# Odd token tiles of the third output-projection part placed between the even tiles of the last part, with both last weight tiles in T3's place

## The chip, the core and the metric

The kernel runs on one core of one Trainium2 chip. The metric is the device time of one execution in microseconds. The kernel before takes 1251.24 us (median of three runs, 1250.85 to 1251.51). In the texts PE is the matrix engine, PEld its weight loads, ACT the scalar engine, DVE the vector engine, POOL the third elementwise engine, and SP the engine on whose queue every DMA is issued.

## What is computed

One decoder layer over 1024 tokens of width 1024, in float32. Cut to what matters here:

```python
mix = jnp.concatenate([oa.reshape(B, S, DIL_WIDTH),
                       ob.reshape(B, S, DIFF_WIDTH)], axis=-1)   # two attentions, 512 columns each
x = x + mix @ w_out[l]                    # output projection, residual
h = rmsnorm(x, g_ffn[l])
gate, up = jnp.split(h @ w_gate_up[l], 2, axis=-1)
x = x + (jax.nn.silu(gate) * up) @ w_down[l]
return rmsnorm(x, g_final)
```

## The kernel before

Every float32 product is done as three products of rounded parts: an operand is split into `h` (rounded) and `l` (the rest), and `h*h + h*l + l*h` is summed in PSUM. A split is a cast on ACT followed by a subtraction on POOL or DVE.

**Output projection.** The 1024 rows of `w_out` are taken in four parts of two 128-row blocks, named by their first block: 4, 6, 0 and 2, in that order. For each part, `mix_tiles` holds the attention's output (`mixh`, `mixl`, two of the four buffers of tag `mix`), and `out_weights` loads the weights for one half `n` of the output columns: a DMA into `raw_o` (one buffer), the cast (L136) and the subtraction (L137). `out_proj_group(mix, w, t, n, name)` does one group: six matmuls of 128x512 for token tile `t` and column half `n`, and an addition to the residual `x1[t]` on DVE (L630). There are 16 groups in each part.

The parts 4, 6 and 0 are generators (`out_proj`) whose groups `mixed` strews between the steps of the last two attention pairs as filler for PE. The scheduler then sets each engine's order from its own estimate of time. Part 2 needs the last attention pair, so it stands behind it, in a region whose PE and POOL order is written out by hand (`manual_schedule`): for the token tiles in the order `TOKENS` = 0, 2, 4, 6, 1, 3, 5, 7, two groups (`n` = 0 and 1, named `op_l`), then the RMSNorm of that tile (`norm`), the store of `x1[t]`, and with a lag of two tiles `flip_low`, which transposes a normalised even tile into `hB[1]` and `hB[2]`, operands of the feed-forward part. That part uses Strassen's seven products, T3 being one of them, and `h7` is the place kept for its operand.

**Norm.** `norm` squares and sums the tile on ACT (L159), takes the power -0.5 on POOL (L145), then scales the low half on DVE (L167). The high half of an even tile goes over ACT (L164) and POOL (L165), of an odd one over DVE (L167).

**Memory near the seam.** The pool `h2T` opens when the attention's pools are closed, and lies on their place. In it, `h1`, `h5`, `h2`, `h3` are operands at once, `h4` and `h6` first hold the split weights of the first gate and up products (`ops0`), and `h7` first holds weights of part 2: before the change those of column half 1 (`wo_l1`); those of half 0 are in two of the four buffers of tag `w`, which frees them when part 0 has used them for half 0. `raw0` (`load_raw`, 1 MB each for gate and up, L729) takes two of the four `mix` buffers, those of part 0.

After the loop, `flip_high` transposes odd tiles and the difference tile `t` (L875 on DVE) into `hB[3]` and `hB[5]`, and `gate_up_first` does the first gate and up products (`pa_g`, `pa_u`), four of 12 matmuls each.

Of the kernel before, what the change touches and what calls it, by code (L numbers as in the profile page):

```python
# [13 lines left out]
F32R = mybir.dt.float32r  # L14
# [5 lines left out]
P = 128  # L20
S = 1024
D = 1024
KT = D // P
# [20 lines left out]
TOKENS = (0, 2, 4, 6, 1, 3, 5, 7)  # L44
# [27 lines left out]
def tile_hybrid_block(  # L72
# [17 lines left out]
    nc = tc.nc  # L90
# [12 lines left out]
    def psum(tag, name):  # L103
        return pp.tile([P, 512], F32, tag=tag, bufs=BANKS[tag], name=name)
# [18 lines left out]
    def split_weights(src, a, name, tag="w", eng=None, parts=None):  # L123

        small = tag == "w"
        pool = wp if small else mapp
        raw = pool.tile([P, 1024], F32, tag="raw" if small else "KL", bufs=1 if small else 2, name=f"raw_{name}")
        nc.sync.dma_start(raw.rearrange("p (a b) -> p a b", a=a), src)
        if parts:
            w = parts  # L130
        elif small:
            w = [pool.tile([P, 1024], F32R, tag=tag, bufs=4, name=f"w_{name}_{i}") for i in "hl"]
        else:
            both = pool.tile([P, 2, 1024], F32R, tag=tag, name=f"w_{name}")
            w = [both[:, i, :] for i in range(2)]
        nc.scalar.copy(w[0], raw)  # L136
        (eng or nc.gpsimd).tensor_tensor(w[1], raw, w[0].bitcast(F32), op=ALU.subtract)  # L137
        return [w_.rearrange("p (a b) -> p a b", a=a) for w_ in w]
# [172 lines left out]
    def chain(*gens):  # L311
        for g in gens:
            yield from g
# [32 lines left out]
    for c in range(3):  # L346
        ps = psum("S", f"gps_{c}")
# [212 lines left out]
    def qk_dil(pair, res):  # L560
        return project_qk(QA + pair * P, KA + pair * P, f"a{pair}", res)

    def qk_diff(h, res):
        return project_qk(QB + h * P, KB + h * P, f"d{h}", res)
# [5 lines left out]
    fill = chain(  # L570
        qk_diff(1, qd[1]),
        project_v(VB + 256, False, "d1", vd2),
        qk_diff(2, qd[2]),
        qk_diff(3, qd[3]),
        project_v(VA, True, "a0", va),
        qk_dil(0, qa[0]),
        qk_dil(1, qa[1]),
        project_v(VA + 256, True, "a1", va2),
# [28 lines left out]
    def mix_tiles(k0):  # L607
        return [mxp.tile([P, 2, S], F32R, tag="mix", name=f"mix{w}_{k0}") for w in "hl"]

    def load_mix(tiles, k0, c):  # L610
        for tl, w in zip(tiles, "hl"):
            nc.sync.dma_start(
                tl[:, :, c * 512 : (c + 1) * 512].bitcast(F32),
                mix_d[w, k0, c].rearrange("k p s -> p k s"),
            )

    n_op = [0]

    def out_proj_group(mix, w, t, n, name):

        sl = slice(t * P, (t + 1) * P)
        cols = slice(n * 512, (n + 1) * 512)
        n_op[0] += name == "l"
        ps = psum("PSPSOS"[n_op[0] % 6] if name == "l" else "P", f"op_{name}_{t}_{n}")
        i = 0
        for k in range(2):
            for l_, r_ in ((mix[0], w[0]), (mix[0], w[1]), (mix[1], w[0])):
                mm(ps, l_[:, k, sl], r_[:, k, :], start=i == 0, stop=i == 5)
                i += 1
        nc.vector.tensor_tensor(x1[t][:, cols], ps, x1[t][:, cols], op=ALU.add)  # L630

    def out_weights(k0, n, parts=None):
        return split_weights(w_out_v[:, k0 : k0 + 2, n * 512 : (n + 1) * 512], 2, f"o{k0}_{n}", parts=parts)

    def out_proj(k0, first=False):
        mix = mix_tiles(k0)
        for c in range(2):
            load_mix(mix, k0, c)
        if first:
            for t in TOKENS:  # L640
                x1[t] = xp.tile([P, D], F32, tag="x1t", name=f"x1_{t}")
                nc.sync.dma_start(x1[t], x[0, t * P : (t + 1) * P, :])
        for n in range(2):
            w = out_weights(k0, n)
            for t in range(KT):
                out_proj_group(mix, w, t, n, f"{k0}")
                yield 1.3

    fill = chain(out_proj(4, True), out_proj(6), out_proj(0))
    mixed(a2, fill, 1.0)  # L650
    mixed(attend_dil(3, qa[3], va2[1]), fill, 1.2)
    run_all(fill)
# [12 lines left out]
    h2p = h2_cm.__enter__()  # L665
# [3 lines left out]
    def h2_tile(i):  # L669
        hB[i] = h2p.tile([P, 2, 4, 512], F32R, tag=f"h{i}", name=f"h2_{i}")  # L670

    wo_l1 = None
    for i in (1, 6, 7, 5, 2, 4, 3):
        if i == 7:
            wo_l1 = h2p.tile([P, 4, 1024], F32R, tag=f"h{i}", name="wo_l1")
        elif i in (4, 6):
            ops0[i == 4] = h2p.tile([P, 4, 2, 512], F32R, tag=f"h{i}", name=f"ops0_{i}")
        else:
            h2_tile(i)
# [9 lines left out]
    def split(src, dst, eng):  # L689

        nc.scalar.copy(dst[:, 0], src)  # L691
        eng.tensor_tensor(dst[:, 1], src, dst[:, 0].bitcast(F32), op=ALU.subtract)  # L692
# [33 lines left out]
    def load_raw(p, up):  # L726
        raw = mxp.tile([P, KT, 256], F32, tag="mix", name=f"raw_{'gu'[up]}{p}")
        c0 = up * D_FF + 2 * p * P
        nc.sync.dma_start(raw, w_gu[:, :, c0 : c0 + 256])  # L729
        return [raw[:, 4 * k : 4 * k + 4, m * P : (m + 1) * P] for m in range(2) for k in range(2)]  # L730

    def as_left(op):
        return op.rearrange("p w (k m) -> p w k m", k=4)
# [132 lines left out]
    def flip_low(j):  # L866
        flip(hns[2 * j][:, LO], 1, j, f"b11_{j}")
        flip(hns[2 * j][:, HI], 2, j, f"b21_{j}")
# [15 lines left out]
        g.tensor_tensor(v[:, LO], u[:, LO], v[:, LO], op=ALU.add)  # L884
        g.tensor_tensor(v[:, HI], v[:, HI], v[:, LO], op=ALU.subtract)

    wo = [out_weights(2, 0), out_weights(2, 1, [wo_l1[:, i] for i in range(2)])]
    mix = mix_tiles(2)
    load_mix(mix, 2, 0)
    gf = mid.tile([P, D], F32, tag="gf", bufs=1, name="gf")  # L890
    nc.sync.dma_start(gf, broadcast(g_ffn[0], D))
    load_mix(mix, 2, 1)
    raw0 = [load_raw(0, up) for up in range(2)]
    a0 = [[as_left(ops0[up][:, i]) for i in range(4)] for up in range(2)]
    with tc.manual_schedule(engines={mybir.EngineType.PE, mybir.EngineType.Pool}):
        for i, t in enumerate(TOKENS):
            for n in range(2):
                out_proj_group(mix, wo[n], t, n, "l")
            high = xp.tile([P, D], F32, tag="x1t", name=f"hn_f{t}") if t % 2 else None
            hns[t] = norm(mid, x1[t], gf, t, "f", high)  # L900
            nc.sync.dma_start(x1_d[t], x1[t])
            if 2 <= i < 6:
                flip_low(i - 2)
            if i >= 3 and i < 7:
                split(raw0[0][i - 3], a0[0][i - 3], nc.gpsimd)
        for i in range(4):
            split(raw0[1][i], a0[1][i], nc.gpsimd)
    with tc.manual_schedule(engines={mybir.EngineType.PE}):
        c0 = [block_tile(0, up) for up in range(2)]
        first = [gate_up_first(up, a0[up], c0[up], c0[0] if up else None) for up in range(2)]  # L910
# [88 lines left out]
    for c0 in range(0, NPAIR - 1, 2):  # L999
# [3 lines left out]
        for i in ORDER:  # L1003
# [14 lines left out]
            for tq in range(4):  # L1018
                ps = next_bank(f"d{c0}_{i}_{tq}")
                sl = slice(tq * P, (tq + 1) * P)  # L1020
                n = 0
# [27 lines left out]
    for m, rows in ((0, (2, 3)), (1, (4, 5))):  # L1049
        for tq in range(4):  # L1050
            sl = slice(tq * P, (tq + 1) * P)
            t = 2 * tq + m
# [4 lines left out]
            for n, r in enumerate(rows):  # L1057
                ps = next_bank(f"dl_{t}_{n}")
                i = 0
                for k in range(2):  # L1060
                    a, w = oal[2 * m + k], wl[2 * k + n]
# [44 lines left out]
```

## Time and profile before

| what | us |
|---|---|
| median of the runs | 1251.24 |
| the profiled execution: its time | 1254.24 |
| the profiled execution: its span | 1252.5 |
| PE busy in the span | 1219.6 |
| the last attention matmul on PE, start | 542.08 |
| the first gate product on PE, start | 586.20 |
| the first up product on PE, start | 602.86 |

The profiled execution is 3.0 us longer than the median, and 1.74 us of it lie outside the span. The page's first part gives busy time by engine, the second part the span in 40 slices with the clock that PE was granted (PEclk, as tenths of full speed). The view of waits says which engine sat idle and what ended it; the timeline gives instructions in order of time, those of one kind that follow each other in one row, with the idle time ahead of it in square brackets; the windows give busy time per engine and the granted clock in a chosen stretch.

### The profile page before, as it was taken

To read this page: it belongs to the slowest core of one execution; us is meant where nothing else is said; L and a number is where in the kernel's file an instruction comes from. 1 tells how busy PE (TensorE), PEld (TensorE's weight loads), DVE (VectorE), ACT (ScalarE), POOL (GpSimd) and SP (SyncE) were. 2 spreads that over 40 slices of the span, in tenths; PEclk is the share of its full clock that TensorE was granted. 3 is DMA by queue.
4 is the path that set the end of the run, shared out by engine and by line. 5 is a ranking of instruction groups with operands and counts; after the bars stand their busy time and mean duration, and the time that the engine had idled before them with its cause. 6 is when DMAs were issued, how large, how long until landed. Compare 5 with 4: busy or idle time off the path is not lost. (4 is left out here: it accounts for less than half of the span.)

```text
span 1252.5 us, 18470 instructions
## 1 busy us (share of the span) xinstructions
PE 1219.6 (97%) x6318; PEld 1040.9 (83%) x6318; DVE 785.4 (63%) x1667; ACT 576.4 (46%) x1300; POOL 737.3 (59%) x664
## 2 busy tenths in 40 slices
PE   6999999999999999998999999999999999999996
PEld 5989989988998888876788888888888887888885
DVE  6548688876766587858554455554545535655597
ACT  5346567665765565535433443434343433222214
POOL 2024344354443443426936797889878786956676
PEclk8999999999999999998999999999999999999999
DMA  6232233132213383252232345333544369966633
GB/s 217 67 89 71 62 98 89 42 93 87 83 51 108 118 307 132 85 173 104 84 121 88 145 169 184 135 120 133 185 168 175 129 244 372 403 230 253 220 126 134
DMA packets 99613, 184.63 MB, mean 147 GB/s; under 512 B 6920, under 2 KB 58376, under 8 KB 99520
## 3 DMA queue, kind: packets, MB, share of 16 engines
q1 hardware_dynamic: 99520, 183.46, 41.9%
q8 instruction: 50, 0.82, 0.3%
q14 instruction: 43, 0.35, 0.1%
HBM read 119.41 MB, written 55.63 MB: 140 GB/s over the span
## 5 line engine op out<-in xcount | busy, mean ns | idle before, releaser
L1024 PE MATMUL d<-wd,oa 128*128 128x512 f32 x840 | 192.9, 391 | 2.8 <-DMA oa<-act_d 2.6
L1024 PEld LDWEIGHTS d<-wd,oa 128*128 128x128 f32 x840 | 158.5, 189 | 36.9 <-ACT acc L1027 3.0
L1029 DVE TENSOR_TENSOR acc<-d,acc 128x512 f32<-128x512 f32 x128 | 86.5, 687 | 62.7 <-PE d L1024 56.6
L547 POOL TENSOR_SCALAR t_a<-t_a,st_a 128x384 f32<-128x384 f32 (+2 forms) x96 | 55.3, 586 | 104.7 <-DVE st_a L443 71.7
L691 ACT CAST wd<-raw_d 128x512 fp32r<-128x512 f32 x74 | 45.1, 622 | 141.7 <-PE d L1024 95.3
L692 POOL TENSOR_TENSOR wd<-raw_d,wd 128x512 fp32r<-128x512 f32 x54 | 73.0, 1372 | 60.6 <-ACT wd L691 60.6
L692 POOL TENSOR_TENSOR ao<-act,ao 128x512 fp32r<-128x512 f32 x52 | 75.3, 1457 | 42.2 <-ACT ao L691 41.8
L692 POOL TENSOR_TENSOR wu<-raw_u,wu 128x512 fp32r<-128x512 f32 x50 | 69.5, 1408 | 29.8 <-ACT wu L691 17.1
L691 ACT CAST wg<-raw_g 128x512 fp32r<-128x512 f32 x70 | 42.2, 620 | 88.8 <-POOL raw_g L705 43.3
L692 POOL TENSOR_TENSOR wg<-raw_g,wg 128x512 fp32r<-128x512 f32 x50 | 75.0, 1517 | 3.2 <-DVE act L797 2.0
L691 ACT CAST wu<-raw_u 128x512 fp32r<-128x512 f32 x70 | 40.6, 619 | 70.7 <-DMA raw_u<-in_w_gate_up 28.4
L433 ACT ACTIVATE t_d<-t_d,st_d 128x384 f32<-128x384 f32 (+3 forms) x96 | 58.5, 612 | 14.4 <-DVE st_d L420 13.9
L433 ACT ACTIVATE t_a<-t_a,st_a 128x384 f32<-128x384 f32 (+2 forms) x96 | 58.7, 613 | 12.6 <-DVE st_a L420 11.9
L458 ACT CAST ath_a<-tp_a 128x384 fp32r<-128x384 f32 (+2 forms) x96 | 45.1, 478 | 41.4 <-PE tp_a L452 40.3
L752 PE MATMUL pc_g<-h,wg 128*128 128x512 f32 x240 | 59.4, 390 | 0.0
L752 PE MATMUL pa_u<-h,wu 128*128 128x512 f32 x240 | 59.3, 392 | 0.0
L752 PE MATMUL pc_u<-h,wu 128*128 128x512 f32 x240 | 59.2, 389 | 0.0
L752 PE MATMUL pa_g<-h,wg 128*128 128x512 f32 x240 | 58.7, 390 | 0.3 <-ACT gate L778 0.3
L752 PE MATMUL pd_u<-h,wu 128*128 128x512 f32 x240 | 58.5, 389 | 0.0
L752 PE MATMUL pd_g<-h,wg 128*128 128x512 f32 x240 | 57.8, 390 | 0.0
L505 POOL TENSOR_SCALAR t_d<-t_d,st_d 128x384 f32<-128x384 f32 (+3 forms) x48 | 30.1, 637 | 46.8 <-DVE st_d L443 32.2
L691 ACT CAST ao<-act 128x512 fp32r<-128x512 f32 x74 | 42.4, 619 | 32.2 <-DVE act L765 12.2
(275 smaller groups left out, 3577.7 us busy)
## 6 DMA issues: line engine op xcount, KB each, us to landing
act_d<-ao SPq DMA_DIRECT2D x74, 512.0 KB, 3.3
oa<-act_d SPq DMA_DIRECT2D x74, 512.0 KB, 4.9
raw_g<-in_w_gate_up SPq DMA_DIRECT2D x11, 1024.0 KB, 5.7
raw_u<-in_w_gate_up SPq DMA_DIRECT2D x11, 1024.0 KB, 6.2
raw_d<-in_w_down SPq DMA_DIRECT2D x11, 1024.0 KB, 10.1
strip<-gtab SPq DMA_DIRECT2D x12, 512.0 KB, 3.7
xt<-in_x SPq DMA_DIRECT2D x8, 512.0 KB, 5.0
raw_o<-in_w_out SPq DMA_DIRECT2D x8, 512.0 KB, 3.8
```

The costliest lines, as they stand in the source:

```text
L433: nc.scalar.activation(tt[:, :n], tt[:, :n], AF.Exp, bias=st[:, last : last + 1], scale=-1.0, accum_out=st[:, 2 + c : 3 + c],)
L458: nc.scalar.copy(hi, pv)
L505: nc.gpsimd.tensor_scalar(t0[:, :n], t0[:, :n], s0[:, 4:5], 1.0, op0=ALU.mult, op1=ALU.mult)
L547: nc.gpsimd.tensor_scalar(t0[:, :n], t0[:, :n], s0[:, 4:5], 1.0, op0=ALU.mult, op1=ALU.mult)
L691: nc.scalar.copy(dst[:, 0], src)
L692: eng.tensor_tensor(dst[:, 1], src, dst[:, 0].bitcast(F32), op=ALU.subtract)
L752: mm(ps, a[:, l_, k, :], b[:, r_, k, :], start=start and i == 0, stop=i == 11, skip_group_check=not start,)
L1024: mm(ps, a[:, l_, sl], w[:, r_, :], start=n == 0, stop=n == 5)
L1029: v.tensor_tensor(acc[i][:, tq], ps, acc[i][:, tq], op=ALU.add)
```

## The change

The third part (block 0) now does only the even token tiles as filler, in the order 0, 2, 4, 6. Its `mix` tiles and both its weights are kept in `rest`. Its odd tiles (`op_h`, eight groups) are placed in the last part's loop, two behind each of the first four (even) tiles. Because part 0's weights stay in the `w` buffers until then, the weights of part 2 go into `h7` for both column halves (`wo_l`). `raw0`, which needs part 0's `mix` buffers, is loaded behind the fourth tile instead of ahead of the loop, its splits begin one tile later, and `flip_low` begins one tile earlier in the loop. Parts 4 and 6 now take their tiles in the order `TOKENS` too. The `op_h` groups join the `op_l` groups in the rotation over PSUM banks.

```diff
-        n_op[0] += name == "l"
-        ps = psum("PSPSOS"[n_op[0] % 6] if name == "l" else "P", f"op_{name}_{t}_{n}")
+        n_op[0] += name in "lh"
+        ps = psum("PSPSOS"[n_op[0] % 6] if name in "lh" else "P", f"op_{name}_{t}_{n}")
...
+    rest = []
+
-    def out_proj(k0, first=False):
+    def out_proj(k0, first=False, tokens=TOKENS):
...
             w = out_weights(k0, n)
-            for t in range(KT):
+            if len(tokens) < KT:
+                rest.append((mix, w))
+            for t in tokens:
...
-    fill = chain(out_proj(4, True), out_proj(6), out_proj(0))
+    fill = chain(out_proj(4, True), out_proj(6), out_proj(0, tokens=TOKENS[:4]))
...
-            wo_l1 = h2p.tile([P, 4, 1024], F32R, tag=f"h{i}", name="wo_l1")
+            wo_l = h2p.tile([P, 4, 1024], F32R, tag=f"h{i}", name="wo_l")
...
-    wo = [out_weights(2, 0), out_weights(2, 1, [wo_l1[:, i] for i in range(2)])]
+    wo = [out_weights(2, n, [wo_l[:, 2 * n + i] for i in range(2)]) for n in range(2)]
...
-    raw0 = [load_raw(0, up) for up in range(2)]
...
-            if 2 <= i < 6:
-                flip_low(i - 2)
-            if i >= 3 and i < 7:
-                split(raw0[0][i - 3], a0[0][i - 3], nc.gpsimd)
+            if i < 4:
+                for n in range(2):
+                    out_proj_group(*rest[n], TOKENS[4 + i], n, "h")
+            if i == 3:
+                raw0 = [load_raw(0, up) for up in range(2)]
+            if 1 <= i < 5:
+                flip_low(i - 1)
+            if i >= 4:
+                split(raw0[0][i - 4], a0[0][i - 4], nc.gpsimd)
```

What that makes of the order, at three places. Names carry part, tile and half (`op_0_7_0` is part 0, tile 7, half 0; `o_a3_3_1` is the last attention output).

**PE behind the attention**, before: the last attention matmul is followed by part 0's odd and even tiles of half 1, with one group of part 2 among them.

```order
L484 MATMUL o_a3_3_1_6681<-atl_a3_3_1_1_6583,Va1_1_4136 128x256
L628 MATMUL op_0_1_1_6760<-w_o0_1_h_6748,mixh_0_6614 128x512
...
L628 MATMUL op_l_0_0_6931<-w_o2_0_h_6909,mixh_2_6917 128x512
L628 MATMUL op_0_2_1_6768<-w_o0_1_h_6748,mixh_0_6614 128x512
...
L628 MATMUL op_l_0_0_6931<-w_o2_0_l_6910,mixh_2_6917 128x512
```

And now: part 2's tile 0 comes at once, and reads `wo_l` in both halves before any `op_h`.

```order
L452 MATMUL tp_a3_7_1_1_6658<-ident_71,t_a3_7_1_1_6643 128x128 x4
L484 MATMUL o_a3_3_1_6681<-ath_a3_3_1_0_6580,Va1_1_4136 128x256
...
L484 MATMUL o_a3_3_1_6681<-atl_a3_3_1_1_6583,Va1_1_4136 128x256
L628 MATMUL op_l_0_0_6861<-wo_l_6763,mixh_2_6851 128x512 x2
...
L628 MATMUL op_l_0_1_6869<-wo_l_6763,mixh_2_6851 128x512 x2
...
L628 MATMUL op_h_1_0_6886<-w_o0_0_h_6622,mixh_0_6614 128x512
```

Seven groups of part 0 that stood behind the attention were PE's work there; now the first two groups are of part 2. The two groups of part 0 that stood between the transposes `tp_a3_7_1` and `o_a3_3_1` are gone from there as well.

**POOL at the same place**, where the second half of each weight split is made. Before:

```order
L137 TENSOR_TENSOR w_o2_0_l_6910<-raw_o2_0_6907,w_o2_0_h_6909 128x1024
L489 TENSOR_SCALAR mh_a3_3_6708<-of_a3_3_6455 128x256
L490 TENSOR_TENSOR ml_a3_3_6709<-of_a3_3_6455,mh_a3_3_6708 128x256
L137 TENSOR_TENSOR wo_l1_6827<-raw_o2_1_6913,wo_l1_6827 128x1024
```

And now:

```order
L489 TENSOR_SCALAR mh_a3_3_6708<-of_a3_3_6455 128x256
L490 TENSOR_TENSOR ml_a3_3_6709<-of_a3_3_6455,mh_a3_3_6708 128x256
L137 TENSOR_TENSOR wo_l_6763<-raw_o2_0_6843,wo_l_6763 128x1024
L137 TENSOR_TENSOR wo_l_6763<-raw_o2_1_6847,wo_l_6763 128x1024
```

The split for half 0 stood ahead of the last attention output's own split (`mh`, `ml`) and now stands behind it. On ACT the casts moved in the same way, from ahead of the copy of `of_a3_3` from `o_a3_3_1` to behind it.

**SP and ACT around the loads.** SP, before:

```order
L128 DMA raw_o2_1_6913<-in_w_out 128x2x512
...
L612 DMA mixh_2_6917<-mixh_d2_1_93 128x2x512
...
L612 DMA mixl_2_6918<-mixl_d2_1_101 128x2x512
L729 DMA raw_g0_6925<-in_w_gate_up 128x8x256
L729 DMA raw_u0_6927<-in_w_gate_up 128x8x256
L901 DMA x1_d_6832<-x1_0_5584 128x1024
```

SP and then ACT, now:

```order
L612 DMA mixl_2_6852<-mixl_d2_1_101 128x2x512
L128 DMA raw_o2_1_6847<-in_w_out 128x2x512
L905 DMA x1_d_6768<-x1_0_5584 128x1024
...
L905 DMA x1_d_6768<-x1_6_5590 128x1024
L734 DMA raw_g0_7053<-in_w_gate_up 128x8x256
L734 DMA raw_u0_7055<-in_w_gate_up 128x8x256
```

```order
L696 CAST ops0_6_6762<-raw_g0_7053 128x512 x2
...
L696 CAST ops0_6_6762<-raw_g0_7053 128x512 x2
L159 ACTIVATE hn_f1_7087,nst_f1_7088<-x1_1_5592 128x1024
...
L696 CAST ops0_4_6766<-raw_u0_7055 128x512 x4
L159 ACTIVATE hn_f3_7127,nst_f3_7128<-x1_3_5594 128x1024
```

The load `raw_o2_1` moved behind the last `mix` load, `raw_g0` and `raw_u0` behind four stores of `x1`, and the casts of `raw_g0` now stand on ACT ahead of the squares of the odd tiles, where before they stood between the squares of tiles 0 and 2.

More of the change, by code (lines that the diff above doesn't have):

```diff
@@ L670, in h2_tile @@
         hB[i] = h2p.tile([P, 2, 4, 512], F32R, tag=f"h{i}", name=f"h2_{i}")
[L672 removed]
+    wo_l = None
     for i in (1, 6, 7, 5, 2, 4, 3):
         if i == 7:
[L675 removed]
+            wo_l = h2p.tile([P, 4, 1024], F32R, tag=f"h{i}", name="wo_l")
         elif i in (4, 6):
```

## The prediction

> **What bounds the kernel now.** First the page, for the share of PE and its clock:
>
> ```profile
> PE 1219.6 (97%) x6318; PEld 1040.9 (83%) x6318; DVE 785.4 (63%) x1667; ACT 576.4 (46%) x1300; POOL 737.3 (59%) x664
> PEclk8999999999999999998999999999999999999999
> ```
>
> PE is busy 97% of the span, so only its idle time and its slow time can be won. The chain of waits reaches back only over the last 24 us and says nothing of this stage. So second, PE's waits from 400 to 620 us:
>
> ```profile
> PE tp_b L856 <- POOL hn_f L165: 4.0, 2, 2.0
> PE tp_b L856 <- DVE h L859: 2.6, 2, 1.8
> ```
>
> PE waits in `flip_low` (`tp_b`) for normalised even tiles. Third, the windows by stage, whose columns are PE, PEld, DVE, ACT, POOL busy, then granted clock, DMA share and GB/s:
>
> ```profile
> 542.40:560.70 18.30, 18.27 (x83) 14.91 (x82) 9.88 (x16) 4.29 (x8) 4.30 (x5) 1.00 0.72 232
> 560.70:575.20 14.50, 9.72 (x36) 7.61 (x37) 8.06 (x14) 10.42 (x19) 7.16 (x8) 0.77 0.40 160
> 586.20:602.90 16.70, 14.88 (x68) 11.88 (x67) 15.59 (x18) 7.17 (x12) 14.72 (x12) 0.90 0.25 90
> ```
>
> Behind the attention PE first runs full for 18 us, then loses idle time and clock while even tiles are flipped, and again while odd ones are. PE's timeline gives the sizes:
>
> ```profile
> 542.08 0.45 PE L484 MATMUL o_a<-atl_a,Va 128*128 128x128 f32 x2
> 542.36 0.40 PE L628 MATMUL op<-w_o_h,mixh 128*128 128x512 f32 x1
> 555.98 0.61 PE L628 MATMUL op_l<-wo_l,mixh 128*128 128x512 f32 x2
> 557.34 0.39 PE L628 MATMUL op_l<-w_o_h,mixh 128*128 128x512 f32 x1
> 562.67 0.66 PE L856 MATMUL tp_b<-ident,hn_f 128*128 128x128 f32 x4 [2.00 <-POOL hn_f L165]
> 566.85 0.63 PE L856 MATMUL tp_b<-ident,hn_f 128*128 128x128 f32 x4 [0.77 <-DVE h L859]
> 569.52 1.11 PE L856 MATMUL tp_b<-ident,hn_f 128*128 128x128 f32 x4 [2.04 <-POOL hn_f L165]
> 575.46 1.03 PE L856 MATMUL tp_b<-ident,hn_f 128*128 128x128 f32 x8
> 576.25 0.48 PE L628 MATMUL op_l<-w_o_h,mixh 128*128 128x512 f32 x1
> 586.20 2.98 PE L752 MATMUL pa_g<-h,ops 128*128 128x512 f32 x12
> 590.99 0.65 PE L856 MATMUL tp_b<-ident,hn_f 128*128 128x128 f32 x4 [1.81 <-DVE h L859]
> 602.86 2.89 PE L752 MATMUL pa_u<-h,ops 128*128 128x512 f32 x12
> ```
>
> A group of six takes 557.34 - 555.98 = 1.36 us, a flip of eight transposes 576.25 - 575.46 = 0.79. From the end of the attention's matmuls at 542.36 to `pa_g` at 586.20 are 43.84 us; in them stand 23 groups (7 of part 0, 16 of part 2: 31.3) and five flips (4.0). So 8.5 us are lost there: 2.00 + 0.77 + 2.04 idle, and the rest in clock and refilling. From `pa_g` to `pa_u` are 16.66 us for 48 matmuls (10.9) and three flips (2.4): 3.3 lost. Together 11.8 us are all that this stage can give.
>
> The clock, by microseconds:
>
> ```profile
> 568.00:569.00 1.00, 0.00 (x0) 0.00 (x0) 0.22 (x1) 1.00 (x3) 0.81 (x1) 0.76 0.89 369
> 575.00:576.00 1.00, 1.00 (x7) 0.79 (x7) 0.67 (x2) 0.00 (x0) 1.00 (x1) 0.83 0.00 0
> 592.00:593.00 1.00, 1.00 (x6) 0.85 (x5) 1.00 (x2) 0.97 (x3) 1.00 (x1) 0.70 0.00 0
> 595.00:596.00 1.00, 1.00 (x4) 0.77 (x4) 1.00 (x2) 0.00 (x0) 1.00 (x2) 0.59 0.00 0
> ```
>
> Between the first two rows the clock is 0.50: PE works at half speed from 569.5 to about 575.2, which costs 5.7/2 = 2.8 us; between the other two some 3 us, so 1.4.
>
> **What the change removes.** Each even tile now has four groups behind it (5.4 us) and more before its flip. Tile 0's second `op_l` group ends 8.2 us (six groups) before its `tp_b`. The norm's long steps, from the groups by line between 540 and 600 us (busy us, mean ns):
>
> ```profile
> L159 ACT ACTIVATE hn_f<-x 128x1024 f32<-128x1024 f32 x8 | 8.5, 1058 | 13.9 <-DVE x L630 9.3 <-issue 4.6
> L164 ACT ACTIVATE hn_f<-x,nst_f 128x512 f32<-128x512 f32 x4 | 2.9, 721 | 1.8 <-POOL nst_f L145 1.8
> L165 POOL TENSOR_TENSOR hn_f<-hn_f,gf 128x512 f32<-128x512 f32 x4 | 5.2, 1294 | 10.0 <-ACT hn_f L164 10.0
> ```
>
> Those are 3.1 us; with DVE's addition, POOL's power and the small steps, each under 0.7, the chain is under 6 us, and the casts of `raw_g` that stood in its way on ACT are gone from there. Tiles 2, 4, 6 have 9.0, 9.0 and 6.3 us. So the three stalls and their clock go: **-8.5 us**. Bound: at least 4.8 (the idle rows), at most 8.5.
>
> **What it adds: the wait for `wo_l`.** This decides. ACT, then POOL, then SP, of before:
>
> ```profile
> 542.56 0.36 ACT L555 COPY of_a<-o_a 64x256 f32<-64x256 f32 x1 [2.43 <-PE o_a L484]
> 546.20 1.05 ACT L136 CAST wo_l<-raw_o 128x1024 fp32r<-128x1024 f32 x1 [3.27 <-DMA raw_o<-in_w_out]
> 540.21 2.40 POOL L137 TENSOR_TENSOR w_o_l<-raw_o,w_o_h 128x1024 fp32r<-128x1024 f32 x1 [9.69 <-ACT w_o_h L136]
> 543.96 0.74 POOL L490 TENSOR_TENSOR ml_a<-of_a,mh_a 128x256 fp32r<-128x256 f32 x1
> 542.64 0.38 SPq L128 DMA_DIRECT2D raw_o<-in_w_out  x1
> 547.59 0.38 SPq L612 DMA_DIRECT2D mixl<-mixl_d  x1
> 552.00:553.00 1.00, 1.00 (x6) 0.84 (x5) 0.69 (x1) 0.00 (x0) 0.00 (x0) 1.00 0.51 197
> ```
>
> In the new order ACT and POOL split half 0's weights only behind the last attention output. Let T be the end of the attention's matmuls (542.36 in the old run). The copy ends at T+0.6, the cast at T+1.7; POOL is through with `ml` at T+2.35 and subtracts until T+4.8. PE's first `op_l` matmul can run at T+1.7, its second, which reads the low part, only at T+4.8. Half 1 is worse: `raw_o` has one buffer, so its load waits for POOL at T+4.8, and on SP stands behind `mixl`, issued at T+5.2 because it waits for the store of the attention output. It goes out at about T+5.65. Alone such a load took 3.56 us (542.64 to 546.20). Here three loads of 512 KB go just ahead of it, and those kept the DMA engines busy until about 552.6 (the last row: half of that microsecond), T+10.2; one more of that size after them gives T+11.6. I take T+11.6, and T+9.2 as the low end. Then the cast (1.05) and the subtraction (2.40): PE can do the second matmul of the second group at T+15.3, and ends that group at T+16.5, where without a wait it would be T+2.7. **+13.8 us**; low end 11.4.
>
> Everything waits behind it: PE's order is fixed, so the `op_h` groups, whose operands have been there for long, stand behind the blocked group, and the norms, flips and the release of `mix` behind them.
>
> **Clock after it.** PE does only eight matmuls in those 15.3 us, so it restarts at half clock. By the row at 569.5 that costs 2.8, by the one at 592 1.4: I take **+2.2**. The Trainium skill (TensorE: Matmul & The Clock Gate, Part 1, What's actually happening) has the array at half rate until one window of about 3.4 us was busy; 3.4/2 would make this term 1.7 by estimate. The trace differs with it in both directions, 5.7 and about 3 us, and the measured rows stand in the sum.
>
> **The last attention output.** The two groups between `tp_a` and `o_a` are gone, so PE meets its own casts: ACT needs 0.6 from the transposes and DVE as much again, against 0.8 us of transposes. **+1.0**, bounds 0.4 to 1.5. That 40 instead of 41 groups stand ahead of T and 24 instead of 23 behind moves 1.36 us from one side to the other: 0.
>
> **The late `raw0`.** It now waits for the last `op_h` matmul, at U. In the old run:
>
> ```profile
> 553.23 0.38 SPq L729 DMA_DIRECT2D raw_g<-in_w_gate_up  x1
> 558.98 1.66 ACT L691 CAST ops<-raw_g 128x512 fp32r<-128x512 f32 x3 [2.23 <-DMA raw_g<-in_w_gate_up]
> 563.31 2.18 ACT L691 CAST ops<-raw_u 128x512 fp32r<-128x512 f32 x4 [0.49 <-DMA raw_u<-in_w_gate_up]
> 585.62 3.45 DVE L167 SCALAR_TENSOR_TENSOR hn_f<-x,nst_f,gf 128x512 f32<-128x512 f32 x2 [0.30 <-POOL nst_f L145]
> 585.56 1.28 POOL L692 TENSOR_TENSOR ops<-raw_g,ops 128x512 fp32r<-128x512 f32 x1
> 586.79 1.74 POOL L885 TENSOR_TENSOR hn_f<-hn_f 128x512 f32<-128x512 f32 x1
> 558.15 0.74 DVE L167 SCALAR_TENSOR_TENSOR hn_f<-x,nst_f,gf 128x512 f32<-128x512 f32 x1
> ```
>
> `raw_g` is there 5.75 us after its issue, `raw_u` after 9.7. ACT stands at the casts of `raw_g` until U+5.9, then does four casts and two flip copies (0.55 each), so the square of tile 1, ready at U+4.4, starts at U+8.7, and its power comes at U+10.7. DVE's products take 0.74 alone and 1.7 each beside these two POOL instructions (the last four rows). Tile 1 is normalised at U+14, `t` at U+15.4. PE has a flip, two groups, a flip and six groups (12.5 us) and waits for about 2.6. Tile 3 follows as late as before, so the old stall of 1.81 there stays. With one more half-clock stretch, less what the old run lost at that place, **+2.2**. Bounds: -3.3 (this stage loses nothing any more) to +4.0.
>
> **Sum**: -8.5 + 13.8 + 2.2 + 1.0 + 2.2 = +10.7. The profiled execution would go from 1254.24 to 1264.9 and its span from 1252.5 to 1263.2. The median is 3.0 below that execution, so 1251.24 + 10.7 = 1261.9; I predict **1261.5**. Ends: all low 11.4 + 1.4 + 0.4 - 8.5 - 3.3 = +1.4; all high 14.5 (a load one microsecond slower still) + 2.8 + 1.5 - 4.8 + 4.0 = +18.
>
> **Rivals.**
>
> 1. *Slower, but by little.* The load of half 1 is not held up by the `mix` loads (T+9.2), and the shift leaves DVE and POOL so much time that the odd tiles never stall. For it: in the old run DVE was busy 15.59 of 16.70 us at the odd flips, and part of that (eight additions of part 0) is now earlier. Against: ACT's order puts `raw_g` ahead of the odd squares. 1251.24 + 11.4 + 1.8 + 0.8 - 8.5 - 2.5 = 1254.2.
> 2. *Faster.* The wait for `wo_l` is not there, because its casts run during the attention: the weights for half 0 lie in `raw_o` long before (POOL had 9.69 us idle ahead of its split). The change then does what its words say: -8.5 + 1.0 and 0 to -3.3 at the odd tiles, 1242 to 1244. It decides once half 1 is split by T+2.7. Against: ACT's copy, POOL's `ml` and a load of at least 3.56 us stand ahead in the orders, and each of these engines works its order through. So T+12.7 (9.2 + 1.05 + 2.40) is a floor from rows.
> 3. *No difference*: the floor of the wait, half clock of 1.4, and nothing lost at all later: within 0.2%, 1252 to 1253.
> 4. *Much slower.* The late `raw0` also delays POOL's splits (1.28 above), so that `pa_g` and `pa_u` wait for `ops0` too: 5 us more, 1267.
>
> **Chances.** The forecast (1257 to 1266) 0.73; rival 1 0.13; rival 4 0.05; rival 3 0.05; rival 2 0.04. The three runs lie within 0.05%, and 0.2% (2.5 us) is about what can be told from no change. Faster 0.04, same 0.05, slower 0.91. The range, with rival 1 in it: 1254 to 1266.
>
> **What would show it.** PE should wait behind `o_a` for ACT's and POOL's `wo_l` (about 5 us), again for the second half (about 9), with PEclk near 0.5 after; no wait of `tp_b` for POOL's `hn_f` at even tiles; ACT idle for `raw_g`, and a wait of PE at the first odd flip. The forecast is wrong if PE meets no `wo_l` wait, or if it waits under 8 us there.

## The result and the profile after

The changed kernel takes 1261.33 us (median of 6 runs, 1259.79 to 1262.73), the kernel before, run beside it, 1252.00 (1250.85 to 1256.94). The ratio is 1.0075, with a 95% interval of 1.0062 to 1.0088: slower by about 9 us. A second series gave 1260.83 against 1250.73, 1.0086 (1.0071 to 1.0101). The forecast was 1261.5, slower. The profiled execution of the changed kernel took 1260.92 us, with a span of 1259.1.

The page's busy times and granted clock, to be held against those of before:

```profile
PE 1219.7 (97%) x6318; PEld 1039.5 (83%) x6318; DVE 786.2 (62%) x1667; ACT 576.5 (46%) x1300; POOL 739.7 (59%) x664
PEclk9999999999999999979999999999999999999999
```

PE is busy for the same 1219.7 us and the span is 6.6 us longer, so what came is idle time. In the 18th slice (535.1 to 566.6 us) the clock is 0.7 now.

PE's waits from 400 to 640 us (waited for, us in total, times, longest):

```profile
PE op_l L628 <- ACT wo_l L136: 7.0, 2, 5.5
PE op_l L628 <- POOL wo_l L137: 4.1, 2, 2.5
PE tp_b L861 <- DVE nst_f L143: 2.0, 1, 2.0
...
PE tp_t L861 <- DVE t L880: 0.4, 1, 0.4
PE o_a L484 <- DVE atl_a L459: 0.3, 1, 0.3
PE o_a L484 <- ACT ath_a L458: 0.2, 1, 0.2
```

The waits of `tp_b` for POOL's `hn_f` at the even tiles are gone, and in their place PE waits 11.1 us for `wo_l`, in two pairs: for ACT's high part, then for POOL's low part, once for each column half. PE's timeline shows where:

```profile
540.34 0.44 PE L484 MATMUL o_a<-atl_a,Va 128*128 128x128 f32 x2
542.30 0.50 PE L628 MATMUL op_l<-wo_l,mixh 128*128 128x512 f32 x1 [1.52 <-ACT wo_l L136]
545.31 0.80 PE L628 MATMUL op_l<-wo_l,mixh 128*128 128x512 f32 x1 [2.50 <-POOL wo_l L137]
...
553.29 0.80 PE L628 MATMUL op_l<-wo_l,mixh 128*128 128x512 f32 x1 [5.48 <-ACT wo_l L136]
555.71 0.79 PE L628 MATMUL op_l<-wo_l,mixh 128*128 128x512 f32 x1 [1.63 <-POOL wo_l L137]
...
558.01 0.63 PE L628 MATMUL op_h<-w_o_h,mixh 128*128 128x512 f32 x1
...
562.39 0.62 PE L628 MATMUL op_l<-wo_l,mixh 128*128 128x512 f32 x2
...
593.20 0.60 PE L861 MATMUL tp_b<-ident,hn_f 128*128 128x128 f32 x4
...
599.65 0.63 PE L861 MATMUL tp_b<-ident,hn_f 128*128 128x128 f32 x4 [2.01 <-DVE nst_f L143]
...
609.93 2.89 PE L757 MATMUL pa_u<-h,ops 128*128 128x512 f32 x12
```

The last attention matmul starts 0.28 us behind the row of 540.34, so T, counted as in the prediction, is 540.62. The second matmul of the first group runs at T+4.7, that of the second group at T+15.1, and the `op_h` groups, whose operands were long there, begin at T+17.4. From the row at 562.39 on, 20 groups and four flips follow without any wait until 593.20. The windows of the three stretches:

```profile
540.60:562.40 21.80, 10.67 (x27) 7.22 (x26) 3.32 (x6) 4.33 (x6) 6.84 (x6) 0.61 0.38 133
562.40:593.20 30.80, 30.80 (x153) 25.78 (x152) 21.11 (x36) 15.82 (x29) 9.36 (x9) 1.00 0.41 154
593.20:609.90 16.70, 14.21 (x73) 11.45 (x72) 16.70 (x22) 8.37 (x14) 15.67 (x12) 1.00 0.23 82
```

Nearly all of the loss lies in the first stretch: PE works there for 10.67 of 21.80 us, at a mean clock of 0.61. The second loses nothing, the third 2.5 us of idle time. The rows of SyncE, ACT and POOL that make the second wait:

```profile
541.21 1.04 ACT L136 CAST wo_l<-raw_o 128x1024 fp32r<-128x1024 f32 x1
542.91 2.34 POOL L137 TENSOR_TENSOR wo_l<-raw_o,wo_l 128x1024 fp32r<-128x1024 f32 x1
545.34 0.42 SPq L128 DMA_DIRECT2D raw_o<-in_w_out  x1
552.19 1.04 ACT L136 CAST wo_l<-raw_o 128x1024 fp32r<-128x1024 f32 x1 [9.94 <-DMA raw_o<-in_w_out]
553.31 2.34 POOL L137 TENSOR_TENSOR wo_l<-raw_o,wo_l 128x1024 fp32r<-128x1024 f32 x1 [8.06 <-ACT wo_l L136]
```

POOL subtracts half 0 until T+4.6, the load of half 1 goes out at T+4.7, is there at T+11.6, and its low part is ready at T+15.0. The load took 6.85 us behind three others of the same size (`mixh`, `gf` and `mixl`), where the same load alone took 3.56 in the kernel before.

For the comparisons below, one table of the stretch from T to the first `pa_u`, worked out from windows of half a microsecond of each profile: idle is the time PE was not busy, half clock is busy time times one minus the granted clock. The stretch holds 21 to 24 groups, depending on how many stand ahead of T, so the last column adds 1.36 us for each group missing from 24.

| kernel | ratio to before (95%) | groups | T to `pa_u` | idle | half clock | at 24 groups |
|---|---|---|---|---|---|---|
| before | 1 | 23 | 60.50 | 6.6 | 4.6 | 61.9 |
| changed | 1.0075 (1.0062 to 1.0088) | 24 | 69.31 | 13.6 | 4.5 | 69.3 |
| changed, second series | 1.0086 (1.0071 to 1.0101) | 24 | 68.89 | 13.4 | 4.4 | 68.9 |
| no wait for `wo_l` | 1.0008 (0.9997 to 1.0020) | 21 | 58.60 | 7.3 | 4.4 | 62.7 |
| the same, no wait for `gf` | 0.9987 (0.9978 to 0.9997) | 21 | 53.98 | 4.8 | 1.7 | 58.1 |
| own buffer for half 1 | 1.0062 (1.0042 to 1.0082) | 24 | 66.00 | 10.7 | 4.1 | 66.0 |
| PE kept busy | 1.0082 (1.0063 to 1.0102) | 24 | 66.57 | 4.6 | 0.0 | 66.6 |
| `op_h` first | 1.0032 (1.0020 to 1.0044) | 21 | 58.55 | 9.0 | 2.2 | 62.6 |
| `op_h` first, own buffer, early splits | 1.0057 (1.0039 to 1.0075) | 21 | 60.85 | 9.8 | 2.9 | 64.9 |
| old order, both weights in T3's place | 0.9997 (0.9987 to 1.0007) | 23 | 57.12 | 5.7 | 1.5 | 58.5 |
| the same, own buffer | 0.9974 (0.9964 to 0.9984) | 23 | 54.56 | 4.7 | 0.0 | 55.9 |
| the same, late `raw0` instead | 1.0012 (1.0003 to 1.0021) | 23 | 59.54 | 6.9 | 2.8 | 60.9 |
| both | 0.9978 (0.9968 to 0.9987) | 23 | 54.73 | 4.8 | 0.0 | 56.1 |
| both, `raw0` a tile earlier | 0.9992 (0.9982 to 1.0001) | 23 | 56.90 | 5.2 | 1.7 | 58.3 |

The traced execution of before is 2 to 3 us above the median of its kernel, and that of the run without a wait for `wo_l` as well (1255.15 for 1252.10); those of the others lie within 1 us of theirs. So these two rows may stand for executions that lost more than usual in this stretch, and where a ratio says something else than they do, the ratio is to be preferred.

### The profile page after: what moved, and what is told of

It reads as the page before. It is cut to its first block, busy times and chain, and to the rows that moved or that the text cites. A ratio compares the mean times of both kernels' runs of the same rounds, so it can differ in the third digit from the quotient of the medians.

```text
span 1259.1 us, 18471 instructions
## 1 busy us (share of the span) xinstructions
PE 1219.7 (97%) x6318; PEld 1039.5 (83%) x6318; DVE 786.2 (62%) x1667; ACT 576.5 (46%) x1300; POOL 739.7 (59%) x664
## 5 line engine op out<-in xcount | busy, mean ns | idle before, releaser
L433 ACT ACTIVATE t_d<-t_d,st_d 128x384 f32<-128x384 f32 (+3 forms) x96 | 58.5, 612 | 14.4 <-DVE st_d L420 13.9
L433 ACT ACTIVATE t_a<-t_a,st_a 128x384 f32<-128x384 f32 (+2 forms) x96 | 58.7, 613 | 12.5 <-DVE st_a L420 11.8
L757 PE MATMUL pd_u<-h,wu 128*128 128x512 f32 x240 | 58.5, 389 | 0.0
```

The source lines that it names most:

```text
L433: nc.scalar.activation(tt[:, :n], tt[:, :n], AF.Exp, bias=st[:, last : last + 1], scale=-1.0, accum_out=st[:, 2 + c : 3 + c],)
L757: mm(ps, a[:, l_, k, :], b[:, r_, k, :], start=start and i == 0, stop=i == 11, skip_group_check=not start,)
```

## The experiments

**Is it the wait for `wo_l`?** First, the changed kernel without that wait.

```diff
-                out_proj_group(mix, wo[n], t, n, "l")
+                out_proj_group(mix, rest[n][1] if i < 3 else wo[n], t, n, "l")
```

> The last-part groups (op_l) of tiles 0, 2 and 4 multiply by part 0's weights, which lie in SBUF long before, in place of part 2's; so these three tiles get a wrong last part, and the number of matmuls stays. No PE instruction before tile 6 then needs wo_l. My theory (the loss is the wait for wo_l with its half clock, and the flip stalls of the old order are won): the 11 us of idle time and the 2.8 of half clock behind the attention go, which leaves the old kernel's time less 8.5 plus 0.6 (o_a meets its casts) less 0.7 (odd flips): 1252.0 - 8.6 = 1243.4, and no wait of PE for wo_l or hn_f between 540 and 580 us. Rival (the new placement itself costs: late raw0, odd groups among even ones): 1252 or more, with stalls elsewhere.

Measured: 1252.10 us, 1.0008 (0.9997 to 1.0020). Some 8 us were won of the 17 to 18 expected. The wait for `wo_l` was gone, but another stood in its place, first on DVE, then on PE:

```profile
555.24 1.84 DVE L167 SCALAR_TENSOR_TENSOR hn_f<-x,nst_f,gf 128x512 f32<-128x512 f32 x1 [2.30 <-DMA gf<-in_g_ffn]
557.23 1.94 PE L861 MATMUL tp_b<-ident,hn_f 128*128 128x128 f32 x8 [3.72 <-DVE hn_f L167]
```

T is 545.30 here, since the free groups let three groups move ahead of it. Tile 0's norm is ready for `gf` at T+7.6, but `gf`, which stands between the loads of `mix` on SyncE, is there only at T+9.9. PE idles for 3.7 us and then loses 2.7 us at half clock. That is 6.4 us of the shortfall of 8.7. The second run takes this operand away as well.

```diff
-            hns[t] = norm(mid, x1[t], gf, t, "f", high)
+            hns[t] = norm(mid, x1[t], x1[7] if i == 0 else gf, t, "f", high)
```

> As the run without a wait for wo_l (tiles 0, 2 and 4 use part 0's weights in their last part), and the norm of tile 0 also multiplies by another tile that lies in SBUF (x1 of tile 7) in place of gf, so that it need not wait for the load of gf; tile 0's hidden state and all that follows from it is then another one. There the first flip waited 3.7 us for a product that waited for gf, and the clock was half for some 6 us behind it. My theory (the new order wins the flip stalls, and what took the gain away was the next operand that comes late, gf): these 3.7 and some 3 us of clock go, the ratio to the kernel before falls from 1.0008 to about 0.9955, 1245.5; what is left of losses are the odd flips. Rival (the first flip comes too early in this order whatever it waits for, or the placement costs elsewhere): 1250 or more.

Measured: 1249.25 us, 0.9987 (0.9978 to 0.9997). From T to `pa_g` PE idles for 2.7 us in all, and the clock stays up:

```profile
544.20:581.30 37.10, 34.37 (x169) 27.57 (x167) 24.19 (x42) 21.16 (x38) 15.63 (x15) 1.00 0.56 195
```

Against the second series of the changed kernel it is 11.6 us faster; in the stretch from T, at equal groups, 10.8. So the wait for `wo_l` and its clock are what makes the changed kernel slow. But it stayed 3.7 us above the 1245.5 expected: without its two late operands the new order wins 1.5 us (0.4 to 2.8) against the old one, not 5 to 6. The 8.5 us that the old trace seemed to promise at the even flips do not show in the whole time.

**Is the second wait the chain of load, cast and subtraction?** The raw weights of half 1 get a place of their own, `h1`, whose operand is not needed yet. The load then also stands ahead of those of `gf` and `mixl` (the cut leaves out the argument `raw`, which hands the place through).

```diff
...
+        elif i == 1:
+            raw_b = h2p.tile([P, 4, 1024], F32, tag="h1", name="raw_b")
...
-    wo = [out_weights(2, n, [wo_l[:, 2 * n + i] for i in range(2)]) for n in range(2)]
+    wo = [out_weights(2, n, [wo_l[:, 2 * n + i] for i in range(2)], raw=raw_b[:, 0] if n else None) for n in range(2)]
+    h2_tile(1)
```

> Only the raw weights of half 1 get a buffer of their own (the place of h2_1, free by then), so their load need not wait until POOL has subtracted half 0; in SyncE's order it now stands behind mixh and ahead of gf and mixl. My theory (the second wait is this chain: buffer, load behind three others, cast, subtraction): with T the end of the attention's matmuls, issue at T+3.7 instead of T+4.7, landing one load behind mixh at T+8 to T+8.7 instead of T+11.5, second matmul of the second group at T+11.5 to T+12.2 instead of T+15.1: 2.9 to 3.6 us faster than the changed kernel, 1258. First wait (T+4.7) unchanged. Rival (the second wait is set by the engines' orders, not by the load): unchanged, 1261.

Measured: 1258.62 us, 1.0062 (1.0042 to 1.0082). T is 540.11 there, and PE's two waits for half 1 read:

```profile
549.93 0.80 PE L629 MATMUL op_l<-wo_l,mixh 128*128 128x512 f32 x1 [2.65 <-ACT wo_l L137]
552.35 0.80 PE L629 MATMUL op_l<-wo_l,mixh 128*128 128x512 f32 x1 [1.63 <-POOL wo_l L138]
```

The second matmul runs at T+12.2 instead of T+15.1, and the stretch is 3.3 us shorter, inside the 2.9 to 3.6 expected. The first wait stayed. The chain is as the prediction had it. By the ratios the whole kernel gained 1.6 to 3.0 us on the two series of the changed one, with an interval of 2.5 us to each side.

**What does the clock cost?** Matmuls that nobody reads fill the two waits.

```diff
+                if i == 0:
+                    for d in range((3, 6)[n]):
+                        keep_busy(f"{n}_{d}")
                 out_proj_group(mix, wo[n], t, n, "l")
```

> 54 matmuls of part 0 whose result nobody reads are added ahead of the first two op_l groups: three groups of six (4.1 us) ahead of the first, six groups (8.2 us) ahead of the second. They fill the two waits for wo_l and end before the second one does, and nothing else changes. My theory (the idle time costs 2.8 us more through the clock): granted clock about 1.00 from T to T+17, the groups behind the wait at 1.36 us from the start, 2.8 us faster than the changed kernel although PE does more: 1258.5. Rival (half clock is not from the idle time, or the matmuls behind the wait are limited by something else): unchanged or slower by what the added groups delay, 1261 to 1263.

Measured: 1260.35 us, 1.0082 (1.0063 to 1.0102), not faster than the changed kernel. The windows from T to the first `op_h`, and of the two `op_h` groups:

```profile
542.50:558.90 16.40, 14.24 (x62) 11.11 (x62) 1.12 (x2) 2.46 (x3) 5.84 (x4) 1.00 0.43 145
558.90:561.60 2.70, 2.70 (x13) 2.23 (x12) 1.44 (x3) 1.15 (x2) 0.25 (x1) 1.00 0.38 156
```

In the stretch the theory holds: the clock stays at 1.00, the two groups take 2.7 instead of 4.4 us, and T to `pa_u` is 2.7 shorter, where 2.8 was expected. The whole time does not show it: T comes 1.85 us later than in the changed kernel, 1.4 of it because one of the added groups was scheduled in among the last `o_a` matmuls:

```profile
540.27 1.55 PE L904 MATMUL warm<-w_o_h,mixh 128*128 128x512 f32 x6
541.66 0.28 PE L484 MATMUL o_a<-atl_a,Va 128*128 128x256 f32 x1
```

**Is it what stands in front of the wait?** All eight `op_h` groups go ahead of the last part, and half 0 of the four even tiles ahead of half 1.

```diff
+        for n in range(2):
+            for t in TOKENS[4:]:
+                out_proj_group(*rest[n], t, n, "h")
+        raw0 = [load_raw(0, up) for up in range(2)]
+        for t in TOKENS[:4]:
+            out_proj_group(mix, wo[0], t, 0, "l")
...
+                flip_low(i - 4)
```

> Same groups, other order: all eight op_h groups first, then the first half of op_l for the four even tiles, then the second half, then the odd tiles, with the even flips between the odd tiles. Three of the op_h groups stand ahead of the last attention output, so nine groups (12.3 us) stand between T and the first matmul that needs half 1 of wo_l, five (6.8 us) before the first that needs half 0. My theory: the wait for half 0 is covered (ready at T+4.7), of the one for half 1 (ready at T+15.1) about 2.5 us stay; 8.6 us of idle time and about 2 of half clock go: 1261.3 - 10.6 = 1250.7. Rival (the groups pile up the additions on VectorE and the casts of raw0 on ScalarE, so the even flips stall as in the old kernel): 1255 to 1259.

Measured: 1254.25 us, 1.0032 (1.0020 to 1.0044): 5 to 7 us won against the changed kernel, not 10.6. The wait for `wo_l` fell from 11.1 to 1.25 us, below the 2.5 worked out. What was lost again stands in PE's timeline and in the windows around it:

```profile
559.51 0.50 PE L628 MATMUL op_l<-wo_l,mixh 128*128 128x512 f32 x1 [1.25 <-POOL wo_l L137]
...
586.52 1.11 PE L861 MATMUL tp_b<-ident,hn_f 128*128 128x128 f32 x4 [4.98 <-DVE h L864]
```

```profile
576.00:584.00 8.00, 5.54 (x33) 4.51 (x31) 7.88 (x13) 5.05 (x9) 7.16 (x9) 1.00 0.24 100
584.00:592.00 8.00, 5.48 (x19) 4.73 (x20) 8.00 (x10) 1.17 (x2) 7.84 (x6) 0.57 0.09 33
```

DVE is busy 15.88 of 16 us and POOL 15.0, and the first odd flip waits 5.0 us for DVE's copy of the flip before it. This is the rival's mechanism, at the odd flips rather than at the even ones. The next run tried to take that load from them.

```diff
-            if i >= 4:
+            if i in (4, 5):
                 flip_low(i - 4)
-                split(raw0[0][i - 4], a0[0][i - 4], nc.gpsimd)
+            if 1 <= i < 5:
+                split(raw0[0][i - 1], a0[0][i - 1], nc.gpsimd)
```

> The order with all op_h first, plus the own buffer for the raw weights of half 1, gf loaded behind mixl, POOL's splits of raw_g beside the even tiles instead of the odd ones, and the last two even flips half a tile earlier. Nine groups (12.3 us) stand between the end of the attention T and the first matmul that needs half 1 of wo_l, which is ready at T+12: no wait for wo_l is left, no half clock there. Against the changed kernel -11.1 - 2.8 us, and up to 3 us given back where ScalarE's casts of raw_g and raw_u stand ahead of tile 0's norm (flip of tile 0 at T+20.4): 1248, between 1246.5 and 1251, a ratio to the kernel before of about 0.997. Rival (as in the run before it, VectorE and GpSimd are the bound around the odd flips, and whatever is won ahead is given back there): 1253 or more.

Measured: 1256.95 us, 1.0057 (1.0039 to 1.0075): the rival's number. No wait for `wo_l` is left, and more is lost at the flips than was won, even ones first, then odd ones:

```profile
569.51 0.66 PE L864 MATMUL tp_b<-ident,hn_f 128*128 128x128 f32 x4 [1.76 <-POOL hn_f L166]
...
585.85 1.09 PE L864 MATMUL tp_b<-ident,hn_f 128*128 128x128 f32 x4 [2.23 <-DVE hn_f L168]
```

It has four edits at once (this one, the own buffer, `gf` behind `mixl`, two even flips half a tile earlier), so which of them cost what is not told apart by it.

**One part of the change alone.** The kernel before, with the weights of both halves in T3's place and its old order.

```diff
-    wo = [out_weights(2, 0), out_weights(2, 1, [wo_l1[:, i] for i in range(2)])]
+    wo = [out_weights(2, n, [wo_l[:, 2 * n + i] for i in range(2)]) for n in range(2)]
```

> One part of the change alone: the kernel before with both halves of the last weights in T3's place, and its old order of groups. The split of half 0 then also waits for the end of the attention T, and the load of half 1 for that split, so half 1 is ready at T+12.7 (high part) and T+15.1 (low part); but seven groups of part 0 (9.5 us) and one op_l group stand behind T ahead of it, so PE reaches it at T+10.9. My theory (the wait is made by the place of the weights, and its size by what stands in front of it): a wait of about 4 us instead of 11, the flip stalls of the old order stay, 0 to 2 us of clock: 1255 to 1258, 1256.5. Rival (the placement is hidden by the seven groups): 1252, no wait for wo_l. Rival (the wait does not depend on the groups in front): 1262.

Beside it ran the changed kernel once more:

> The changed kernel once more, beside the others of this call, so that they can be compared on one chip. Ratio to the kernel before 1.0075 again (1.0062 to 1.0088), some 1260.5; the same waits for wo_l.

Measured: 1250.14 us, 0.9997 (0.9987 to 1.0007), beside 1.0086 for the whole change on the same chip. PE's timeline:

```profile
554.67 0.50 PE L628 MATMUL op_l<-wo_l,mixh 128*128 128x512 f32 x1 [1.60 <-ACT wo_l L136]
557.10 0.80 PE L628 MATMUL op_l<-wo_l,mixh 128*128 128x512 f32 x1 [1.92 <-POOL wo_l L137]
566.16 0.66 PE L856 MATMUL tp_b<-ident,hn_f 128*128 128x128 f32 x4 [0.31 <-POOL hn_f L165]
570.24 0.63 PE L856 MATMUL tp_b<-ident,hn_f 128*128 128x128 f32 x4 [0.24 <-DVE h L859]
```

The wait is 3.5 us, as worked out from the seven groups in front of it (about 4). Yet the time did not rise by the 4 to 7 us of my theory (1255 to 1258, beside 1250.73 for the kernel before). The even flips, which idled 4.8 us before, now idle 0.55. This is the main thing that I had wrong: **the wait and the flip stalls are not two terms of a sum.** In the kernel before, ACT casts `raw_g` until 560.6, ahead of tile 0's scaling, and tile 0's flip starts at 562.7, 2.0 us after PE was there; a wait of PE ahead of it uses up the same time.

**Do the two losses hide one another?** The old order with both weights in T3's place, then with the own buffer for half 1 (a shorter wait), with `raw_g` and `raw_u` held back on SyncE (ACT free for the norms), and with both. The second edit:

```diff
-    raw0 = [load_raw(0, up) for up in range(2)]
...
-    with tc.manual_schedule(engines={mybir.EngineType.PE, mybir.EngineType.Pool}):
+    with tc.manual_schedule(engines={mybir.EngineType.PE, mybir.EngineType.Pool, mybir.EngineType.SP}):
...
+            if i == 2:
+                raw0 = [load_raw(0, up) for up in range(2)]
```

> The kernel before with both last weights in T3's place (the old order of groups), and the raw weights of half 1 in a buffer of their own, so that half 1 is ready at T+12 instead of T+15.1. PE reaches it at T+11. Without the own buffer PE waited 3.5 us there and lost 1.6 us to half clock, but its even flips, which lose 4.8 us of idle time and some 3 us of clock in the kernel before, then lost only 0.6. My new theory (the flips do not wait for PE's own work but for ScalarE's, whose casts of raw_g and raw_u stand ahead of the norms; a wait of PE ahead of them uses up the same time, so the two losses are not added): the wait for wo_l falls to about 1 us, and the even flips stall again by 2 to 4 us: 1249 to 1251, no change to the kernel before. Rival (two separate losses): the wait goes and the flips stay quiet, 1246.

Measured: 1247.20 us, 0.9974 (0.9964 to 0.9984), between theory and rival, and **faster than both kernels**.

```profile
552.91 0.50 PE L629 MATMUL op_l<-wo_l,mixh 128*128 128x512 f32 x1 [0.60 <-POOL wo_l L138]
561.43 0.66 PE L859 MATMUL tp_b<-ident,hn_f 128*128 128x128 f32 x4 [1.21 <-POOL hn_f L166]
566.69 0.65 PE L859 MATMUL tp_b<-ident,hn_f 128*128 128x128 f32 x4 [1.13 <-POOL hn_f L166]
```

The wait fell by 2.9 us and its half clock (1.5) went; 1.8 us came back at the even flips. So they hide one another in part.

> The kernel before with both last weights in T3's place, and the loads of raw_g and raw_u held back in SyncE's order until tile 4's store, so ScalarE's casts of them no longer stand ahead of the even tiles' norms. The wait for half 1 of wo_l (3.5 us) is left as it is. My new theory (the wait of PE and the busy ScalarE hide in one another): nearly nothing is won, since the even flips hardly stall any more with the wait in front: 1249 to 1250.5. Rival (ScalarE's casts cost by themselves): 1247 or less.

Measured: 1251.80 us, 1.0012 (1.0003 to 1.0021). The rival (1247 or less) falls, and the theory's 1249 to 1250.5 was too low as well: by the ratios the kernel loses some 2 us against the one without the late loads. Not all of it need be theirs. Of the 2.4 us by which its stretch is longer, 1.3 are half clock behind the wait for `wo_l` (2.8 us, where the other trace has 1.5), a wait that is as long as there (3.4 and 3.5 us) and comes ahead of the flips. The rest lies at the flips: ACT's casts of `raw_g` now stand ahead of tile 6's scaling and of the copy of the flip before it, and PE idles at tile 6's flip for 0.56 and 0.90 us:

```profile
572.52 2.18 ACT L691 CAST ops<-raw_g 128x512 fp32r<-128x512 f32 x4 [0.83 <-DMA raw_g<-in_w_gate_up]
574.61 0.72 ACT L164 ACTIVATE hn_f<-x,nst_f 128x512 f32<-128x512 f32 x1
```

> Both: own buffer for the raw weights of half 1, and raw_g and raw_u held back until tile 4's store, in the old order of groups. My new theory (either alone wins nothing, both together win what the two stalls cover): the wait for wo_l about 1 us, no half clock behind it, even flips without a stall; the odd flips' 1.7 us stay: 1250.1 - 2.5 - 1.6 - 0.5 = 1245.5, a ratio of 0.996 to the kernel before. Rival (VectorE and GpSimd are the bound up to the odd flips, and take it back there): 1249 or more.

> As the run with both edits, with raw_g and raw_u held back one tile less, until tile 2's store (2.7 us earlier), so that GpSimd's splits of raw_g come further ahead of the odd tiles' norms, which they slow on VectorE. ScalarE's casts of raw_g then stand ahead of the norm of tile 6 only. 1245 to 1246.5; if the odd flips lose less than the 1.7 us of before, 1244.

Measured: 1248.13 us, 0.9978 (0.9968 to 0.9987), and 1248.69, 0.9992 (0.9982 to 1.0001). Both have no half clock up to `pa_g`, and neither beats the own buffer alone: the flips of the even tiles wait 1.9 and 2.3 us for DVE's copies now, and the second odd flip 2.0 and 2.2. My second theory, that both edits together win what the stalls cover, falls: the late loads only move the stall from one flip to another.

## Why the prediction was right, and where it was not

The direction, the place and the time came out: 1261.33 for 1261.5. By its steps, with the profiled execution:

- **The wait for `wo_l`, +13.8, and the clock, +2.2.** Right. T+4.8, T+11.6 and T+15.3 were worked out; T+4.7, T+11.6 and T+15.1 are in the rows above. The first matmul of tile 2, the second in the order, starts 16.3 us later than 4 groups behind T would (562.39 against 540.62 + 5.45), for 16.0 in the sum. Of it the group that ends the wait ran at half clock already, and the two `op_h` groups took 4.4 instead of 2.7. Shortening the load won 3.3 us in the stretch and keeping the clock up 2.7, each where and as large as expected from this step. Taking away the wait, and that for `gf` with it, won 11 us, 5 less than the step has, in part because other losses came in its place: PE waits 0.92 us for DVE's `of_a` behind the attention and 0.65 at tile 0's flip there, and half clock behind the second odd flip costs 1.69 us where the changed kernel lost none.
- **The flip stalls, -8.5.** They are gone: 20 groups and four flips take 30.8 us, for 30.4 by their lengths, so -8.1 against the trace of before. But the step's reason was incomplete. It gave the gain to the longer distance between norm and flip; in the trace of the run with the old order and the same weights, a wait of 3.5 us ahead of the flips goes with 4.3 us less of the 4.8 us of idle time. So a stall ahead on the same path takes time off the next one, and in the changed kernel, with 11 us of waiting in front, the old distances might have sufficed too, which no run shows. Without the two late operands the order won only 1.5 us.
- **The last attention output, +1.0.** 0.24 + 0.34 = 0.58 us; right, within its bounds.
- **The late `raw0`, +2.2.** This step failed: from the first odd flip to `pa_u` the changed kernel takes 16.73 us (593.20 to 609.93), the kernel before 17.45, so the stretch is 0.7 us shorter, not 2.2 longer. The first odd flip of before:

```profile
585.41 0.60 PE L856 MATMUL tp_b<-ident,hn_f 128*128 128x128 f32 x4
```

And the rows of the changed kernel:

```profile
580.50 0.38 SPq L734 DMA_DIRECT2D raw_g<-in_w_gate_up  x1
588.38 1.06 ACT L159 ACTIVATE hn_f<-x 128x1024 f32<-128x1024 f32 x1
590.38 1.30 POOL L697 TENSOR_TENSOR ops<-raw_g,ops 128x512 fp32r<-128x512 f32 x1
591.25 1.65 DVE L167 SCALAR_TENSOR_TENSOR hn_f<-x,nst_f,gf 128x512 f32<-128x512 f32 x2
594.23 1.29 POOL L888 TENSOR_TENSOR hn_f<-hn_f 128x512 f32<-128x512 f32 x1 [2.54 <-issue]
```

With U at 580.5, tile 1's square starts at U+7.9 (8.7 was taken), and its two products take 1.65 us together, not 1.7 each: POOL, which slows them, is idle from 591.7 to 594.2. `t` is ready 1.8 us earlier than worked out, and PE waits 0.44 us instead of 2.6. The Trainium skill (SBUF — State Buffer, Who interferes with whom) says that a VectorE instruction with two inputs in SBUF and a GpSimd instruction that reads SBUF contend for one port, and that one blocks until the other is done; the trace agrees in that the two products took 1.65 us here, and 3.45 where POOL worked beside them in the kernel before. Nor did the second stall, of 2.01 us, bring half clock this time, where the kernel before lost 1.71 us to it at this place (the prediction read 1.4). Half clock there comes and goes with no cause that the runs show, so this much of the term is luck: with it the term would have been about +1.0.

- **The sum and the median.** By the profiled executions the terms are -8.1 + 16.3 + 0.6 - 0.7 = +8.1, for +10.7. The executions themselves differ by 6.7: the attention ends 1.0 us earlier than one group less and the +0.6 make it, and 0.4 is won behind `pa_u`, both outside the sum. So the sum was 4.0 us too high, and that the time came out to 0.2 us all the same is largely luck: I took the 3.0 us by which the traced execution of before lay above its median over to the changed kernel, whose traced execution lies 0.4 below its median. Where the traced execution of before lost them, one trace cannot tell.
- **The rivals.** That the wait is not there, or that the loads do not hold up half 1, is refuted by the rows, and no difference by the ratio. The waits of `pa_g` and `pa_u` for `ops0`, of the fourth rival, are not in PE's list. The floor of T+12.7 for half 1 held only while its load waits for the one buffer: with an own buffer half 1 was ready at T+12.2, and at T+11.8 in the old order.

## What to carry to other kernels

A weight that is split only behind a serial stage needs other work in front of its first use, work that waits neither for that stage nor for that weight. When an order is changed to remove one stall, count what stood in front of the next late operand before and after. Two stalls on one path are not simply added: shorten the first, and see how much of the second comes back, before either is given a price. A buffer that a load waits for can be found in the trace, since the load goes out right behind the last reader (at 545.34 us here, POOL being through at 545.25); an own place for it made the fastest kernel here (0.9974), where no change of order alone that kept all operands beat the kernel before.

## What the hardware showed that I had not expected

- **Half clock behind a long wait.** The granted clock fell to 0.50 some 3.8 us behind T (a mean of 0.71 from 544 to 545 us), stayed there over a burst of five matmuls (545.3 to 547.8) and a single one at 553.3, and came back 5.8 us after PE was busy without a break (from 555.7 on; the mean is 0.76 from 561 to 562):

```profile
544.00:545.00 1.00, 0.00 (x0) 0.00 (x0) 0.00 (x0) 0.00 (x0) 1.00 (x1) 0.71 0.40 80
545.00:546.00 1.00, 0.69 (x2) 0.60 (x3) 0.00 (x0) 0.00 (x0) 0.25 (x1) 0.50 0.59 193
...
561.00:562.00 1.00, 1.00 (x5) 0.81 (x4) 1.00 (x2) 0.73 (x1) 0.16 (x2) 0.76 0.03 8
```

- **Half clock behind a short one.** At the second odd flip PE stalls for about 2 us in nearly every kernel here. In before (1.81 us), in the two runs without a wait for `wo_l` (2.05, 2.06) and in the one with both edits and `raw0` a tile earlier (2.15) it was followed by a loss of 1.69 to 1.71 us by half clock; in eight others (1.63 to 2.04) by none. So neither the length of the stall alone nor the kernel's median decides it. The Trainium skill (TensorE: Matmul & The Clock Gate, Part 1, What's actually happening) has a free-running window of 3.41 us; half of that is 1.71 by estimate, and the trace agrees with this size (1.69 to 1.71). The same section has the clock fall after an idle window of that length, and there the trace differs: stalls of 1.81 to 2.15 us were enough. Whether the phase of the window decides which stall drops the clock was not tested.
